# A mixture of experts that returns every expert's rows by one-hot products, with the rows for its gathers written through GpSimd's queue

## The chip, the cores and the metric

The kernel runs on one core of a Trainium2 chip. The core has a matrix engine (TensorE, PE in the rows), a vector engine (VectorE, DVE), a scalar engine (ScalarE, ACT), a general engine (GpSimd, POOL) and a sync engine (SyncE, SP) that only issues transfers. Transfers can be issued from SP's, ACT's and POOL's queues and run on 16 DMA engines. The metric is the device time of one execution in microseconds.

## The reference, cut to what matters

One layer on 512 tokens (and 16 meta tokens) of width 1,024: a mixer of two attention branches, then a mixture of 32 experts in which each token goes to two experts of one group, then a final norm. All arithmetic is float32.

```python
u = rmsnorm(h, norm_ffn_g)                  # 512 x 1024
g_sel = top_1(softmax(u @ w_group + b_group))
e_sel = top_2(softmax((u @ w_router + b_router) of that group))
gate  = p_grp * p_exp / sum(p_exp)
for each expert e, on the rows of u that chose it:
    hid = silu(x @ w1[e]) * (x @ w3[e])     # 1024 -> 512
    y   = hid @ w2[e]                       # 512 -> 1024
    out[token] += y * gate
h = h + out
return rmsnorm(h, norm_final_g)
```

## The kernel before, in words

The first half (to about 500 us) is the mixer; its instructions are placed by a scheduler that orders them by a modelled time. The rest is the expert stage, where the order of TensorE, ScalarE and VectorE is the order of the code.

Before the experts, `router_half` (L849) runs for each of the four blocks b of 128 tokens and each half nh of the width, as soon as that half of the residual stream h is done. GpSimd multiplies it by the norm's weights (L854), and ACT's queue writes the result u2 to a table `u2d` in memory (L855), eight writes of 256 KB. `choose` (L877) picks the experts, `few_rows` (L1036) makes the row indices of the first pair of experts, and `gather` (L1053) fetches those rows of `u2d` into a tile X by an indirect transfer from GpSimd's queue. Meanwhile `tables` (L945) works out, by small one-hot products, the tables for all pairs: which token sits in which slot, its gate and its norm factor. `busy` (L930) gives TensorE idle products to do in between.

Each expert has 64 slots. Two experts share one gather of 128 slots; slots that hold no token are skipped by the bounds check. The loop in `stage_moe` (L1146) runs over 32 experts, in 16 pairs, and `expert` (L1171) is one step of it: in four parts g it takes two weight pieces each and multiplies (`up_step`, L1110), and between them it does the expert before: transposes its hidden rows (L1123) and multiplies them by four w2 pieces (`down_piece`, L1131). In odd steps X is transposed for the next pair (L1095). A step reads 12 weight pieces of 512 KB, all through SP's queue, into rings of tiles: 24 tiles "R", 11 tiles "W", and 5 tiles "P" once at the start. SP issues them up to 35 pieces ahead, and each waits until the tile it goes to has been read by TensorE.

What an expert gives back goes one of two ways. `FAR = 12`: the first 12 experts (six pairs) are `far` (L1206): ScalarE and VectorE scale the two halves of the product by the gate into a tile, and for each pair `scatter` (L1066) writes its rows by an indirect transfer to a table `y2d` in memory, one row for each token and choice. The table is cleared early in the mixer by `clear_far` (L1058), four writes of 1 MB through SP's queue. `fetch_far` (L1072), at step 13, reads all of `y2d` back in eight transfers of 512 KB into eight R tiles, and step 16 adds them to h (L1196). The later 20 experts are `near` (L1232): GpSimd builds the one-hot matrix ST of tokens and slots (L1084), ScalarE and VectorE scale and split the product into a tile Y of two parts (L176, L177), and in every second step `arrived` (L1218) multiplies Y by ST for each block of 128 tokens (`to_tokens`, L1144) and adds the sums to h (L1225). ST takes a W tile, Y a P tile.

`ending` (L1240) finishes the last pair, the final norm and the output.

Of the kernel before, what the change touches and what calls it, by code (L numbers as in the profile page):

```python
# [9 lines left out]
F32 = mybir.dt.float32  # L10
# [13 lines left out]
NB = 4  # L24
# [42 lines left out]

GATES_A = [4, 4, 4, 4]
TOPK = [(3,), (2,), (1, 0), ()]
FAR = 12  # L70


class Body:
# [106 lines left out]
    def setup(self):  # L180
        nc, a = self.nc, self.a
        nc.scalar.preload_act_table_set("natural_log_exp_and_others")
        cs = self.C([128, C_ONCE], F32, "const")
        nc.scalar.dma_start(cs, a["consts"][:, 0:C_ONCE])
        self.cs = cs
        self.idt = cs[:, C_ID:C_ID + 128]
        self.idb = self.C([128, 128], BF16, "idb")
        nc.vector.tensor_copy(self.idb, self.idt)
        once = self.H([128, C_N - C_ONCE], F32, "once")
        nc.scalar.dma_start(once, a["consts"][:, C_ONCE:C_N])  # L190
        for k, (name, dt) in enumerate((("maskb", BF16), ("srope", F32R))):
            t = self.C([128, 128], dt, name)
            nc.vector.tensor_copy(t, once[:, 128 * k:128 * k + 128])
            setattr(self, name, t)
        self.tokb = self.C([128, 8], BF16, "tokb")
        nc.vector.tensor_copy(self.tokb, cs[:, C_TOKB:C_TOKB + 8])
        self.nhalf = self.C([128, 1], F32, "nhalf")
        nc.gpsimd.memset(self.nhalf, -0.5)
        self.gat = [self.dr.tile([128, 8, 512], F32, name=f"gate{i}", tag=f"gate{i}") for i in range(2)]

        self.u2d = self.dr.tile([T, D], F32, name="u2d", tag="u2d")
        self.y2d = self.dr.tile([2 * T, D], F32, name="y2d", tag="y2d")
        win = a["w_in"].rearrange("(c p) n -> p c n", p=128)

        def unit(*cols, eng=None):
            for kh in range(2):
                pc, at = [], 0
                for c0, n in cols:
                    pc.append((lambda t, at=at, n=n: t[:, :, at:at + n],
                               win[:, 4 * kh:4 * kh + 4, c0:c0 + n]))  # L210
                    at += n
                self.queue([128, 4, 256], *pc, how=dict(n=at) if at < 256 else dict(eng=eng))

        def unit128(c0):
            self.queue([128, 8, 128], (lambda t: t, win[:, :, c0:c0 + 128]), how=dict(eng=nc.gpsimd) if c0 >= O_GA else None)

        unit((O_CKV, 144), (O_KI, 72))
        unit((O_QI, 256), eng=nc.gpsimd)
        unit((O_QI + 256, 256), eng=nc.gpsimd)
        unit128(O_QA)  # L220
        unit128(O_KA)
        unit((O_VA, 256))
        unit((O_VA + 256, 256))
        self.gate_n = 0
        n = 0

        def gates(k):
            nonlocal n
            for i in range(n, n + k):
                unit128((O_GA if i < 8 else O_GB) + 128 * (i % 8))  # L230
            n += k

        def ups(w):
            v = a[w].rearrange("(c p) n -> p c n", p=128)
            for nh in range(2):
                for kp in range(2):
                    self.queue([128, 2, 512], (lambda t: t, v[:, 2 * kp:2 * kp + 2, 512 * nh:512 * nh + 512]))
                yield

        for g in range(4):  # L240
            if g < 3:
                unit128(O_QA + 128 * (g + 1))
                unit128(O_KA + 128 * (g + 1))
            else:
                unit((O_QB, 256))
                unit((O_QB + 256, 256))
            gates(GATES_A[g])
        ua = ups("w_up_a")
        for g in range(4):
            if g < 2:  # L250
                next(ua)
        ub = ups("w_up_b")
        next(ub)
        next(ub)
        v = a["w_o"].rearrange("(c p) n -> p c n", p=128)
        for nh in range(2):
            for kp in range(4):
                self.queue([128, 2, 512], (lambda t: t, v[:, 2 * kp:2 * kp + 2, 512 * nh:512 * nh + 512]))
        self.expert_at = len(self.loads)
        pcs = [self.expert_pieces(a["w1"][e], a["w3"][e], a["w2"][e]) for e in self.experts()]  # L260
        order = []
        for e in range(NE):
            last = iter(pcs[e - 1][8:] if e > 0 else [])
            for g, c in enumerate(self.spread(e)):
                order += pcs[e][2 * g:2 * g + 2]
                order += [next(last) for _ in range(c)]
        order += pcs[NE - 1][8:]
        for i, (shape, src) in enumerate(order):
            self.queue(shape, (lambda t: t, src), tile=self.home(i))
# [579 lines left out]
    def router_half(self, b, nh, h):  # L849
# [2 lines left out]
        cols = slice(512 * nh, 512 * nh + 512)  # L852
        u2 = self.H([128, 512], F32, "u2")
        nc.gpsimd.tensor_tensor(u2, h, self.g2[:, cols], ALU.mult)  # L854
        nc.scalar.dma_start(self.u2d[128 * b:128 * b + 128, cols], u2)  # L855
        junk = self.A([128, 512], F32, "junk")
        nc.scalar.activation(junk, h, AF.Square, accum_out=self.ss[:, b, nh:nh + 1])
        p = self.tr()
# [86 lines left out]
    def tables(self, d):  # L945
# [14 lines left out]
        den = self.S([128, NB], F32, "den", bufs=1)  # L960
        nc.vector.tensor_tensor(den, s[:, :, 0], s[:, :, 1], ALU.mult)
        nc.vector.reciprocal(den, den)
        self.vec = self.S([128, NB, 2, 4], F32, "vec", bufs=1)
        tok = cs[:, C_TOK:C_TOK + 8].rearrange("p (k b) -> p b k", k=2)
        nc.scalar.activation(self.vec[:, :, :, 0], tok[:, :, 0:1].to_broadcast([128, NB, 2]), AF.Copy)
        nc.scalar.activation(self.vec[:, :, :, 2], self.rs.unsqueeze(2).to_broadcast([128, NB, 2]), AF.Copy)
        nc.scalar.activation(self.vec[:, :, :, 3], tok, AF.Copy)
        nc.vector.tensor_tensor(self.vec[:, :, :, 1], d[:, :, 4:6], den.unsqueeze(2).to_broadcast([128, NB, 2]), ALU.mult)
        io = cs[:, C_I128:C_I128 + 128]
        n = [128, 8, 4, 16]  # L970
        cv = self.H(n, F32, "cv")
        nc.vector.tensor_tensor(cv, self.cb.unsqueeze(2).to_broadcast(n),
                                self.vec.rearrange("p b k n -> p (b k) n").unsqueeze(3).to_broadcast(n), ALU.mult)
        tp = self.av()[:, 0:64]
        for q in range(2):
            rh = self.H([128, 4, 128], F32, "rowoh")
            n = [128, 4, 128]
# [17 lines left out]
        nc.vector.tensor_scalar(it, self.tab[:, 0], 0.0, 4095.0, op0=ALU.is_equal, op1=ALU.mult)  # L995
        self.idx = self.C([128, 16], I32, "idx")
        nc.vector.scalar_tensor_tensor(self.idx, self.tab[:, 0], -1.0, it, op0=ALU.add, op1=ALU.add)
        self.idy = self.C([128, 16], I32, "idy")
        nc.vector.scalar_tensor_tensor(self.idy, tp[:, 48:64], -1.0, it, op0=ALU.add, op1=ALU.add)

    def overflow(self):

# [50 lines left out]
    def gather(self, x, ix, n):  # L1053
        self.nc.gpsimd.indirect_dma_start(  # L1054
            out=x[0:n], out_offset=None, in_=self.u2d[:, :],
            in_offset=bass.IndirectOffsetOnAxis(ap=ix, axis=0), bounds_check=T - 1, oob_is_err=False)

    def clear_far(self):  # L1058

        z = self.R([128, D], F32, "z")  # L1060
        self.nc.gpsimd.memset(z, 0.0)
        y = self.y2d.rearrange("(p a) d -> p a d", a=8)
        for a in range(0, 8, 2):
            self.nc.sync.dma_start(y[:, a:a + 2, :], z.unsqueeze(1).to_broadcast([128, 2, D]))

    def scatter(self, y, p):  # L1066

        self.nc.gpsimd.indirect_dma_start(
            out=self.y2d[:, :], out_offset=bass.IndirectOffsetOnAxis(ap=self.idy[:, p:p + 1], axis=0), in_=y,
            in_offset=None, bounds_check=2 * T - 1, oob_is_err=False)  # L1070

    def fetch_far(self):  # L1072

        self.back = []
        for b in range(NB):
            for k in range(2):
                t = self.R([128, D], F32, "back")
                r = T * k + 128 * b
                self.nc.gpsimd.dma_start(t, self.y2d[r:r + 128, :])
                self.back.append((self.h[b], t))  # L1080

    def tokens(self, tk, st):

# [62 lines left out]
    def stage_moe(self):  # L1146
        nc = self.nc
        self.hT = [self.H([128, 4, 64], F32, "hT") for _ in range(2)]
        with self.tc.manual_schedule(engines={nc.tensor.engine, nc.scalar.engine, nc.vector.engine}):
# [5 lines left out]
            xs = self.x_copy(self.x_turn(self.X[0]))  # L1155
            hid, self.kept = None, []
            for e in range(NE):
                if e == FAR + 1:
                    self.fetch_far()
                if e == NE - 2:  # L1160
                    self.gf = self.A([128, D], F32, "gfin")
                    nc.gpsimd.dma_start(self.gf, self.a["norm_final_g"].partition_broadcast(128))
# [8 lines left out]
    def expert(self, e, xs, hid):  # L1171
# [8 lines left out]
        for g, k in enumerate(self.spread(e)):  # L1180
# [10 lines left out]
                c += 1  # L1191
            if len(self.kept) == 2:
                self.arrived((g + 2) % 4)
            if e == FAR + 4:
                for h, back in self.back[2 * g:2 * g + 2]:
                    nc.vector.tensor_tensor(h, back, h, ALU.add)  # L1196
            if e == NE - 1 and g == 2:
                self.last = {2: (self.av(), self.mm())}
                self.stay(2)
        if len(self.kept) == 2:  # L1200
            self.kept = []
        if c == 4:
            (self.far if e - 1 < FAR else self.near)(o, e - 1)
        return nx, hid

    def far(self, o, e):  # L1206

        p, r = divmod(e, 2)
        if r == 0:
            self.y = self.P([128, D], F32, "far")  # L1210
        y = self.y[64 * r:64 * r + 64]
        gate = self.gate[:, r, p:p + 1]
        self.nc.scalar.activation(y[:, 0:512], o[0:64], AF.Copy, scale=gate[0:64])
        self.nc.vector.tensor_scalar(y[:, 512:], o[64:128], gate[64:128], None, op0=ALU.mult)
        if r:
            self.scatter(self.y, p)

    def arrived(self, b):  # L1218

# [136 lines left out]
def block_kernel(ctx: ExitStack, tc: tile.TileContext, **aps):  # L1356
# [6 lines left out]
    hp = tc.high_priority  # L1363
    aw = s.a_weights(*s.a_qk())
    s.a_values()
    s.clear_far()
    for g in range(4):
        if g < 3:
            nxt = s.a_weights(*s.a_qk())
# [59 lines left out]
```

## Time and profile before

| | us |
|---|---|
| median of 3 runs | 1030.07 (1025.9 to 1030.82) |
| the profiled execution: its time | 1029.66 |
| its span, first to last instruction | 1027.9 |
| TensorE busy | 912.8 (89% of the span) |
| VectorE busy | 514.4 (50%) |
| ScalarE busy | 340.5 (33%) |
| GpSimd busy | 203.6 (20%) |

The span is what the profile's rows are counted in; the execution's own time lies 1.8 us above it. A busy TensorE is not one at its peak, and a share over the whole span mixes stages with different limits, so the stage of the experts, from about 500 us on, is read by itself. In a row "x8" is a count, and `[3.26 <-DMA X<-u2d,ixr]` at its end says that the engine stood idle that long before it and what released it. Tile names are those of the program without buffer numbers: raw is a weight piece, X the gathered rows, mm, tr and av are tiles of the matrix engine's output memory.

### The profile page before, as it was taken

The page shows a single profiled execution, that of the slowest core. Times are in us where ns is not written, and L with a number is a line of the kernel's source. Part 1 is how long each engine was busy: PE and PEld are TensorE (multiplying, and loading weights), DVE is VectorE, ACT ScalarE, POOL GpSimd, SP SyncE. Part 2 cuts the span into 40 slices and gives each one's busy share as a digit, 9 for nine tenths or more (in the row PEclk, how much of TensorE's full clock was granted, in tenths as well). Part 3 has the DMA queues.
Part 4 walks back from the last instruction along what each step waited for, and adds up shares of the span by engine and source line. Part 5 has one row for each costly group of instructions (what it writes and reads, how often), then busy time and mean ns, then how long its engine had stood idle before and what let it go on. Part 6 is the DMA issues. An engine that isn't in the chain of part 4 may idle for free.

```text
span 1027.9 us, 13393 instructions
## 1 busy us (share of the span) xinstructions
PE 912.8 (89%) x4862; PEld 567.7 (55%) x4863; DVE 514.4 (50%) x1021; ACT 340.5 (33%) x670; POOL 203.6 (20%) x232
## 2 busy tenths in 40 slices
PE   6989999899998989889789998878749999989994
PEld 5877897778896878668543332223213433333331
DVE  7559999997827679584521141110234322223232
ACT  6156645567645576452101111111101111111113
POOL 4220042514250100252210000002212011111201
PEclk8899899899999999999889999999969999999998
DMA  9000062314433134388679999999999999999962
GB/s 318 20 21 21 22 225 62 103 42 123 131 90 103 44 110 145 81 299 311 263 285 417 416 416 416 418 417 415 414 417 417 414 415 416 416 415 417 416 281 83
DMA packets 112021, 263.57 MB, mean 256 GB/s; under 512 B 17341, under 2 KB 49349, under 8 KB 111953
## 3 DMA queue, kind: packets, MB, share of 16 engines
q1 hardware_dynamic: 95296, 237.89, 59.8%
q10 hardware_dynamic: 12192, 14.32, 4.2%
q0 software_dynamic: 4464, 10.48, 2.7%
q8 instruction: 39, 0.64, 0.2%
q14 instruction: 30, 0.24, 0.1%
HBM read 252.70 MB, written 15.73 MB: 261 GB/s over the span
## 4 chain that ended last, share of the span: by engine, by line
PE 44%; DMA 31%; DVE 15%; issue 3%; ACT 3%; POOL 3%; ACTq 0%; DVEq 0%; SPq 0%; POOLq 0%
DMA raw<-in_w 28%; PE mm L1110 11%; PE mm L1131 5%; PE mm L381 4%; PE mm L392 4%; PE mm L811 3%; PE mm L779 3%; PE mm L1144 3%; DVE E L680 2%; DVE score L548 2%; PE av L593 2%; PE mm L500 2%; DVE m L547 2%; PE mm L501 1%; DVE w L168 1%
## 5 line engine op out<-in xcount | busy, mean ns | idle before, releaser
L1110 PE MATMUL mm<-raw,xs 128*64 128x512 f32 x1024 | 249.9, 605 | 21.2 <-DMA raw<-in_w 20.9
L1110 PEld LDWEIGHTS mm<-raw,xs 128*64 128x64 f32 x1024 | 68.1, 137 | 157.5 <-issue 111.1
L1131 PE MATMUL mm<-raw,hT 128*64 128x512 f32 x512 | 130.1, 602 | 26.1 <-DMA raw<-in_w 25.6
L392 PE MATMUL mm<-uH,w 128*128 128x512 f32 (+1 forms) x448 | 129.9, 370 | 2.9 <-DVE w L168 2.7
L1116 DVE SCALAR_TENSOR_TENSOR hid<-mm,rss,g 64x512 f32<-64x512 f32 x32 | 23.8, 743 | 190.3 <-ACT g L1114 190.3
L1114 ACT ACTIVATE g<-mm,rss 64x512 f32<-64x512 f32 x32 | 21.9, 684 | 227.8 <-PE mm L1110 227.8
L1225 DVE TENSOR_TENSOR h<-mm,h 128x512 f32<-128x512 f32 x72 | 46.4, 686 | 94.0 <-PE mm L1144 94.0
L392 PEld LDWEIGHTS mm<-uH,w 128*128 128x128 f32 x448 | 81.6, 191 | 17.4 <-DVE w L168 3.1
L381 PE MATMUL mm<-w,uH 128*128 128x256 f32 (+1 forms) x448 | 86.8, 295 | 1.5 <-ACT nat L467 1.1
L1131 PEld LDWEIGHTS mm<-raw,hT 128*64 128x64 f32 x512 | 34.1, 137 | 95.0 <-issue 47.0
L392 PE MATMUL mm<-uL,w 128*128 128x512 f32 (+1 forms) x224 | 82.9, 371 | 0.0
L381 PEld LDWEIGHTS mm<-w,uH 128*128 128x128 f32 x448 | 74.2, 203 | 2.8 <-ACT nat L467 1.6
L381 PE MATMUL mm<-w,uL 128*128 128x256 f32 (+1 forms) x224 | 65.9, 294 | 2.6 <-DVE uL L174 2.6
L167 ACT ACTIVATE w<-raw 128x1024 fp32r<-128x1024 f32 (+1 forms) x54 | 55.5, 1048 | 15.0 <-DMA raw<-in_w_in 10.3
L1084 POOL TENSOR_SCALAR ST<-route,tks 128x512 fp32r<-128x512 f32 x20 | 33.1, 1662 | 131.6 <-PE mm L1110 72.7
L168 POOL TENSOR_TENSOR w<-raw,w 128x1024 fp32r<-128x1024 f32 x20 | 48.5, 2438 | 46.1 <-ACT w L167 16.2
L1054 POOL DMA_INDIRECT X<-u2d,idx x15 | 15.5, 1035 | 204.9 <-PE tr L1095 154.1
L1144 PE MATMUL mm<-Y,ST 64*128 64x512 f32 x308 | 51.6, 424 | 0.0
L168 DVE TENSOR_TENSOR w<-raw,w 128x1024 fp32r<-128x1024 f32 (+1 forms) x34 | 46.8, 1388 | 6.3 <-ACT w L167 5.5
L381 PEld LDWEIGHTS mm<-w,uL 128*128 128x128 f32 x224 | 45.3, 202 | 3.0 <-DVE uL L174 3.0
L392 PEld LDWEIGHTS mm<-uL,w 128*128 128x128 f32 x224 | 42.7, 191 | 6.8
L1144 PEld LDWEIGHTS mm<-Y,ST 64*128 64x128 f32 x308 | 30.5, 190 | 26.9 <-issue 16.2
(333 smaller groups left out, 1493.7 us busy)
## 6 DMA issues: line engine op xcount, KB each, us to landing
raw<-in_w SPq DMA_DIRECT2D x384, 512.0 KB, 10.0
raw<-in_w_in SPq DMA_DIRECT2D x36, 512.0 KB, 4.1
y2d<-z SPq DMA_DIRECT2D x4, 1024.0 KB, 9.0
gate<-gst ACTq DMA_DIRECT2D x16, 256.0 KB, 2.7
gate<-gate ACTq DMA_DIRECT2D x8, 512.0 KB, 6.4
raw<-in_w_o SPq DMA_DIRECT2D x8, 512.0 KB, 5.2
back<-y2d POOLq DMA_DIRECT2D x8, 512.0 KB, 16.6
x<-in_x SPq DMA_DIRECT2D x4, 512.0 KB, 5.8
```

Source lines behind the costliest of these rows:

```text
L167: nc.scalar.activation(h, r, AF.Copy)
L168: (eng or nc.vector).tensor_tensor(l, r, h.bitcast(F32), ALU.subtract)
L381: nc.tensor.matmul(o, s, m[:, c % 4, :n], start=(c == 0 and k == 0), stop=(c == 7 and k == 2))
L392: nc.tensor.matmul(p[:, :x1 - x0], s[:, c, :], m, start=(c == 0 and k == 0), stop=(c == 7 and k == 2))
L779: nc.tensor.matmul(p, s, y[c][:, m, :], start=(c == 0 and k == 0), stop=(c == 3 and k == 2))
L811: nc.tensor.matmul(p, s, m[:, c % 2, :], start=(c == 0 and k == 0), stop=(c == 7 and k == 2))
L1084: self.nc.gpsimd.tensor_scalar(st, self.io512, tk, None, op0=ALU.is_equal)
L1110: self.nc.tensor.matmul(p[r:r + 64], xs[:, k, par], w[:, c, :], start=(k == 0), stop=(k == 7))
L1116: self.nc.vector.scalar_tensor_tensor(hid, p[0:64], rs[0:64], g1, op0=ALU.mult, op1=ALU.mult)
L1131: self.nc.tensor.matmul(o[64 * n:64 * n + 64], ht[:, c, :], w2[:, 0, 512 * n:512 * n + 512], start=(c == 0), stop=(c == 3))
L1144: self.nc.tensor.matmul(ps[n], st[r, 128 * b:128 * b + 128], y[r, j, :], start=(first and j == 0), stop=(last and j == 1))
L1225: self.nc.vector.tensor_tensor(h, ps[n], h, ALU.add)
```

## The change

`FAR` and the three functions of the way through memory go: no clearing, no scatter, no reading back, no fourth column in the tables (the row of `y2d` that a slot goes to). All 32 experts are `near`. The eight writes of u2 move from ACT's queue to GpSimd's.

```diff
-FAR = 12
...
-        self.y2d = self.dr.tile([2 * T, D], F32, name="y2d", tag="y2d")
...
         nc.gpsimd.tensor_tensor(u2, h, self.g2[:, cols], ALU.mult)
-        nc.scalar.dma_start(self.u2d[128 * b:128 * b + 128, cols], u2)
+        nc.gpsimd.dma_start(self.u2d[128 * b:128 * b + 128, cols], u2)
...
-        self.vec = self.S([128, NB, 2, 4], F32, "vec", bufs=1)
+        self.vec = self.S([128, NB, 2, 3], F32, "vec", bufs=1)
...
-        nc.scalar.activation(self.vec[:, :, :, 3], tok, AF.Copy)
...
-        self.idy = self.C([128, 16], I32, "idy")
-        nc.vector.scalar_tensor_tensor(self.idy, tp[:, 48:64], -1.0, it, op0=ALU.add, op1=ALU.add)
...
-                if e == FAR + 1:
-                    self.fetch_far()
...
-            if e == FAR + 4:
-                for h, back in self.back[2 * g:2 * g + 2]:
-                    nc.vector.tensor_tensor(h, back, h, ALU.add)
...
         if c == 4:
-            (self.far if e - 1 < FAR else self.near)(o, e - 1)
+            self.near(o, e - 1)
...
-    s.clear_far()
```

Three places show how instructions move. The first is the last write of u2. On ScalarE before, with what each instruction waits for, the program's last two writes stand between the squares of L857 and the exponential of the gates; DMAHW2 is a count of finished transfers, and Pool and DVE count those engines' instructions.

```order
L857 ACTIVATE junk_5098,ss_4729<-h_4706 128x512 [waits DVE_49,Activation_49]
L855 DMA u2d<-u_5095 128x512 [waits DMAHW5_49,Pool_49]
L857 ACTIVATE junk_5147,ss_4729<-h_4708 128x512 [waits DVE_49,Activation_49]
L855 DMA u2d<-u_5144 128x512 [waits DMAHW2_49,Pool_49]
L942 ACTIVATE gd_5243<-gd_5243 128x24 [waits DVE_49]
```

On GpSimd in the changed kernel the same two writes stand behind the product that makes their data, and the first gather behind them.

```order
L852 TENSOR_TENSOR u_5088<-h_4699,gffn_4703 128x512 [waits DMAHW7_49,DMAHW0_49,DVE_49]
L871 TENSOR_TENSOR rs_4723<-ms_5105,nhalf_95 128x1 [waits DVE_49]
L853 DMA u2d<-u_5088 128x512 [waits Pool_49]
L852 TENSOR_TENSOR u_5137<-h_4701,gffn_4703 128x512 [waits DMASW0_49,DVE_49]
L853 DMA u2d<-u_5137 128x512 [waits Pool_49]
L871 TENSOR_TENSOR rs_4723<-ms_5154,nhalf_95 128x1 [waits DVE_49]
L1048 DMA X_4724<-u2d,ixr_5218 128x1024 [waits DMASW4_49,DMASW5_49,DMASW3_49,DMASW6_49,DMASW2_49,DMASW7_49,DMASW1_49,DVE_49]
```

The writes lost their wait for a DMAHW count. SP's weight loads of the kernel before use the same eight counts in turn; the one on DMAHW2 that is issued last ahead of that write is the first of these rows.

```order
L140 DMA raw_5376<-in_w 128x1024 [waits DMAHW2_49]
L140 DMA raw_5382<-in_w 128x1024 [waits DMAHW3_49]
L140 DMA raw_5392<-in_w 128x1024 [waits DMAHW4_49]
L140 DMA raw_5364<-in_w 128x1024 [waits DMAHW5_49,PE_49]
L140 DMA raw_5366<-in_w 128x1024 [waits DMAHW6_49,PE_49]
```

In the changed kernel the loads on SP keep these counts, without the eight writes of u2 between them.

The second place is TensorE at the start of the fourth expert's step. Before, the transposes of the expert before it are followed by the next two weight pieces.

```order
L1110 MATMUL mm_5562<-raw_5376,xs_5452 64x512
L1123 MATMUL tr_5571<-const_83,hid_5547 128x64 x4
L1110 MATMUL mm_5562<-raw_5382,xs_5452 64x512
L1110 MATMUL mm_5562<-raw_5380,xs_5452 64x512
...
L1095 MATMUL tr_5586<-const_83,X_4731 128x128 x4
```

In the changed kernel (L1080 is L1110 there, L1093 is L1123, L1114 is L1144) eight products to the tokens stand between them (four rows are shown), and so in all four parts of every second step from here on.

```order
L1080 MATMUL mm_5553<-raw_5366,xs_5442 64x512
L1093 MATMUL tr_5562<-const_83,hid_5539 128x64 x4
L1114 MATMUL mm_5569<-Y_5483,ST_5481 128x512
L1114 MATMUL mm_5570<-Y_5483,ST_5481 128x512
...
L1114 MATMUL mm_5569<-Y_5550,ST_5481 128x512
L1114 MATMUL mm_5570<-Y_5550,ST_5481 128x512
...
L1080 MATMUL mm_5553<-raw_5372,xs_5442 64x512
```

That is 32 products for each of the six pairs that were far. The third place is GpSimd's queue in the first steps: before, gathers of X and scatters to y2d.

```order
L1054 DMA X_4732<-u2d,idx_5302 128x1024 [waits DMASW1_49,PE_49]
L1068 DMA y2d<-far_5491,idy_5304 1024x1024 [waits DVE_49]
L1054 DMA X_4731<-u2d,idx_5302 128x1024 [waits DMASW2_49,PE_49]
L1068 DMA y2d<-far_5635,idy_5304 1024x1024 [waits DMASW4_49,DVE_49]
L1054 DMA X_4732<-u2d,idx_5302 128x1024 [waits DMASW3_49,PE_49]
```

In the changed kernel (L1048 is the gather, L1054 the one-hot matrix) the scatters' places hold two matrices for each pair, which wait for TensorE to leave a W tile.

```order
L1048 DMA X_4725<-u2d,idx_5294 128x1024 [waits DMASW1_49,PE_49]
L1054 TENSOR_SCALAR ST_5481<-route,tks_5279 128x512 [waits DMAHW6_49,PE_49]
L1054 TENSOR_SCALAR ST_5481<-route,tks_5279 128x512
L1048 DMA X_4724<-u2d,idx_5294 128x1024 [waits DMASW2_49,PE_49]
L1054 TENSOR_SCALAR ST_5674<-route,tks_5279 128x512 [waits DMAHW5_49,PE_49,Activation_49]
L1054 TENSOR_SCALAR ST_5674<-route,tks_5279 128x512
```

In the mixer the scheduler places a few dozen instructions of TensorE and VectorE earlier or later by some rows, and the weight splits on GpSimd by one or two; none is added there.

## Rows read from the trace of the kernel before

**Rows 1.** The page: what the DMA engines moved in 40 equal slices of the span.

```profile
GB/s 318 20 21 21 22 225 62 103 42 123 131 90 103 44 110 145 81 299 311 263 285 417 416 416 416 418 417 415 414 417 417 414 415 416 416 415 417 416 281 83
```

**Rows 2.** Busy time by stretch: length; PE, PEld, DVE, ACT, POOL; granted clock; DMA share; GB/s.

```profile
130.00:160.00 30.00, 28.64 (x208) 26.25 (x207) 29.14 (x69) 14.97 (x31) 13.67 (x10) 1.00 0.50 182
...
540.00:560.00 20.00, 20.00 (x96) 7.11 (x94) 3.00 (x4) 3.50 (x6) 1.01 (x1) 1.00 1.03 417
...
720.00:760.00 40.00, 20.04 (x96) 7.35 (x92) 6.79 (x10) 3.04 (x5) 5.41 (x9) 0.77 1.03 415
760.00:800.00 40.00, 40.00 (x199) 15.61 (x199) 20.69 (x24) 5.18 (x9) 9.33 (x5) 0.97 1.03 417
...
960.00:1000.00 40.00, 36.67 (x178) 13.00 (x174) 10.08 (x15) 4.89 (x8) 6.19 (x4) 1.00 0.86 351
```

**Rows 3.** The timeline of ACT: the gate (L1114) of experts 1, 7, 18, 24, 31.

```profile
543.85 0.68 ACT L1114 ACTIVATE g<-mm,rss 64x512 f32<-64x512 f32 x1 [5.18 <-PE mm L1110]
...
614.35 0.68 ACT L1114 ACTIVATE g<-mm,rss 64x512 f32<-64x512 f32 x1 [5.19 <-PE mm L1110]
...
800.24 0.68 ACT L1114 ACTIVATE g<-mm,rss 64x512 f32<-64x512 f32 x1 [6.33 <-PE mm L1110]
...
884.87 0.68 ACT L1114 ACTIVATE g<-mm,rss 64x512 f32<-64x512 f32 x1 [6.61 <-PE mm L1110]
...
997.30 0.69 ACT L1114 ACTIVATE g<-mm,rss 64x512 f32<-64x512 f32 x1 [12.03 <-PE mm L1110]
```

**Rows 4.** The chain that ended last: start, length, what.

```profile
739.18 19.14 DMA raw<-in_w
...
982.23 1.94 PE mm L1110 x8
```

**Rows 5.** DMA: one queue's packets, megabytes and share; issues, KB each, median us to landing.

```profile
q0 software_dynamic: 4464, 10.48, 2.7%
...
back<-y2d POOLq DMA_DIRECT2D x8, 512.0 KB, 16.6
...
u2d<-u ACTq DMA_DIRECT2D x8, 256.0 KB, 6.7
...
gfin<-in_norm_final_g POOLq DMA_DIRECT2D x1, 512.0 KB, 7.1
...
X<-u2d,idx POOLq DMA_INDIRECT x15, 7.1
```

**Rows 6.** The timeline from the last u2 to the first expert.

```profile
502.60 1.27 POOL L854 TENSOR_TENSOR u<-h,gffn 128x512 f32<-128x512 f32 x1 [4.78 <-issue]
...
509.91 0.33 ACTq L855 DMA_DIRECT2D u2d<-u  x1
...
511.75 0.16 DVE L1050 TENSOR_SCALAR ixr<-av 128x1 int32<-128x1 f32 x1 [0.47 <-PE av L1048]
...
517.67 1.29 POOL L1054 DMA_INDIRECT X<-u2d,ixr  x1 [12.26 <-DMA raw<-in_w]
...
518.36 1.89 PE L934 MATMUL mm<-route,idb 128*128 128x512 bf16 x8
...
523.51 1.97 PE L1095 MATMUL tr<-const,X 128*128 128x128 f32 x8 [3.26 <-DMA X<-u2d,ixr]
```

**Rows 7.** Busy time by stretch, as in Rows 2, around the first expert's start.

```profile
522.00:524.00 2.00, 0.49 (x3) 0.49 (x4) 0.00 (x0) 0.00 (x0) 0.00 (x0) 0.86 0.52 150
524.00:526.00 2.00, 2.00 (x9) 1.37 (x10) 0.48 (x1) 0.60 (x1) 0.25 (x1) 0.50 0.00 0
526.00:528.00 2.00, 2.00 (x10) 0.65 (x8) 0.21 (x1) 0.00 (x0) 0.75 (x1) 0.79 0.29 49
```

**Rows 8.** Groups by line: busy, mean ns of one, idle time before and its releasers.

```profile
L1225 DVE TENSOR_TENSOR h<-mm,h 128x512 f32<-128x512 f32 x72 | 46.4, 686 | 94.0 <-PE mm L1144 94.0
...
L1084 POOL TENSOR_SCALAR ST<-route,tks 128x512 fp32r<-128x512 f32 x20 | 33.1, 1662 | 131.6 <-PE mm L1110 72.7
L168 POOL TENSOR_TENSOR w<-raw,w 128x1024 fp32r<-128x1024 f32 x20 | 48.5, 2438 | 46.1 <-ACT w L167 16.2
```

More of the change, by code (lines that the diff above doesn't have):

```diff
@@ L962, in tables @@
         nc.vector.reciprocal(den, den)
-        self.vec = self.S([128, NB, 2, 4], F32, "vec", bufs=1)
-        tok = cs[:, C_TOK:C_TOK + 8].rearrange("p (k b) -> p b k", k=2)
-        nc.scalar.activation(self.vec[:, :, :, 0], tok[:, :, 0:1].to_broadcast([128, NB, 2]), AF.Copy)
+        self.vec = self.S([128, NB, 2, 3], F32, "vec", bufs=1)
+        nc.scalar.activation(self.vec[:, :, :, 0], cs[:, C_TOK:C_TOK + NB].unsqueeze(2).to_broadcast([128, NB, 2]), AF.Copy)
         nc.scalar.activation(self.vec[:, :, :, 2], self.rs.unsqueeze(2).to_broadcast([128, NB, 2]), AF.Copy)
-        nc.scalar.activation(self.vec[:, :, :, 3], tok, AF.Copy)
         nc.vector.tensor_tensor(self.vec[:, :, :, 1], d[:, :, 4:6], den.unsqueeze(2).to_broadcast([128, NB, 2]), ALU.mult)
         io = cs[:, C_I128:C_I128 + 128]
-        n = [128, 8, 4, 16]
+        n = [128, 8, 3, 16]
         cv = self.H(n, F32, "cv")
@@ L973, in tables @@
                                 self.vec.rearrange("p b k n -> p (b k) n").unsqueeze(3).to_broadcast(n), ALU.mult)
-        tp = self.av()[:, 0:64]
+        tp = self.av()[:, 0:48]
         for q in range(2):
@@ L1056, in gather @@
             in_offset=bass.IndirectOffsetOnAxis(ap=ix, axis=0), bounds_check=T - 1, oob_is_err=False)
[L1058 to L1080, printed above, removed]
     def tokens(self, tk, st):
@@ L1202, in expert @@
         if c == 4:
-            (self.far if e - 1 < FAR else self.near)(o, e - 1)
+            self.near(o, e - 1)
         return nx, hid
[L1206 to L1216, printed above, removed]
     def arrived(self, b):
```

## The prediction

> **What bounds the kernel now.** I read the bytes by slice first. Up to about 500 us they jump between 20 and 311 GB/s; from the 22nd slice to the 38th they stand at 414 to 418 [rows 1]. So the expert stage is to be looked at as a stream. The stretches say how full it is: DMA share 1.03 at 415 to 417 GB/s at 540 us, at 720 and at 760, that is, from about 540 to past 960, while TensorE is busy for 40 of 40 us in one stretch and for 20 of 40 in another [rows 2]. TensorE's load changes and the stream's doesn't: the stream sets the end. The chain agrees: it holds a wait of 19.14 us for one weight piece at 739 us, and its last wait for a weight ends at 982.23 us [rows 4]. From there on TensorE runs without one, 45.7 us to the end of the span (1027.9); I take that tail as it is.
>
> The reader should see a second thing, since it decides how safe the first is: TensorE's own pace where nothing is late. From expert 1 to 7, all far, the gates are 70.50 us apart, 23.50 a pair. From expert 18 to 24, all near, 84.63 us, 28.21 a pair [rows 3]. The stream needs more: 24 pieces of 0.524 MB and on average 64 gathered rows of 4 KB (1,024 rows in 16 gathers, two for each token) are 12.84 MB, at 416.5 GB/s 30.8 us a pair. A near pair still fits under it, by 2.6 us; a far pair by 7.3.
>
> **The way through memory: what leaves the stream.** GpSimd's queue moved 10.48 MB [rows 5]. Eight reads of y2d at 0.524 MB are 4.19, the final norm's weights 0.52, the gathers 1,024 x 4,096 bytes = 4.19. What is left, 1.57 MB, is what the six scatters wrote. The change takes 4.19 + 1.57 = 5.76 MB out of a stream that runs at 416.5 GB/s: **13.8 us**. All of it counts, because the stream is full at both places, also where the reads of y2d hold TensorE up (half busy from 720 to 760 us, clock 0.77) and where it catches up after [rows 2].
>
> **What it costs TensorE and the others.** Six pairs go from 23.50 to 28.21 us, 28 us of work in all. It lies under the stream as long as TensorE keeps ahead. Without any wait, expert 31's gate would come 15 pairs of 28.21 us after expert 1's, at 543.85 + 423.2 = 967.0 us; the stream brings it today at 997.30 [rows 3] and then at about 983. TensorE has 16 us in hand, about 1.1 us a pair. VectorE adds 48 more sums to h of 0.69 us, GpSimd 12 more one-hot halves of 1.66 us [rows 8]; in the near stretch VectorE is busy for 20.7 of 40 us and GpSimd for 9.3 [rows 2], and they do it there at the pace of 28.21, so this hides too. GpSimd's one-hot matrix can wait for a W tile, and the next gather stands behind it; near pairs have both in that order already, so I price it at nothing, and with the cover gone at what a pair then takes over 29.3 us.
>
> **The tiles.** ST now takes W tiles from the first pair on, so fewer weights can be under way. The near stretch at 760 us lives with that at 417 GB/s [rows 2]: nothing. The eight R tiles for y2d come free.
>
> **The last write of u2.** The last product of u2 ends at 502.60 + 1.27 = 503.87 us, but its write is issued at 509.91 [rows 6]. ScalarE's queue has nothing to do then; the write waits for the count of a weight load (the order of the change section shows DMAHW2). It lands at 517.67, when the gather that waited for it starts, although its indices were ready at 511.9. The gather lands 5.84 us later; TensorE, done with its idle products at 518.36 + 1.89 = 520.25, starts on X at 523.51, 3.26 us late. From GpSimd's queue the write has no such wait and goes out at about 505, counting 1.3 us for the issue like the gather's. Its landing has no row, so I bound it: 6.7 us, the median of these writes from ScalarE's queue, and 16.6, that of the eight reads of y2d, eight at once, on GpSimd's; the gathers there take 7.1 [rows 5]. One write of 256 KB is nearest to the gather: landing at 512, gather from 512 to 518, before TensorE is ready at 520.25. Landing counts only beyond 514.4. So TensorE gains 3.3 us, in the other bound (landing at 521.6) it loses 3.9.
>
> The idle gap also costs clock: after it the granted clock is 0.50 (1.2 GHz) to 526 us and 0.79 to 528 [rows 7]; over the 0.6 us that the first expert runs to 526 and the next 2 that is 0.3 + 0.4 = 0.7 us. Without the gap I count it back. These **4.0 us** reach the end only if the stream starts earlier with TensorE, and it does: the tiles are full, and DMA stands at shares of 0.52, 0.00 and 0.29 in these six us, 4.4 us of idle time, until the first expert's tiles come free [rows 7].
>
> Here a rule of the Trainium skill stands against the row. Its page "DMA: Bandwidth & Descriptors", section "Issuing engines are not separate DMA queues", says that transfers from any engine's queue run on the same 16 DMA engines, so another queue only saves the time to initiate them, usually a small thing. By that alone this term would be near 0 and the whole 13.8; by the row, the 6 us between data and issue are no matter of bandwidth and can go, so I keep the 4.0.
>
> **The rest.** The seven other writes add some 0.6 to 1.3 us each to GpSimd between products 7 us apart: hidden. One table column, one copy and one index operation leave the start, under 0.4 us: not counted. The clearing of y2d lies where VectorE is busy for 29.14 of 30 us and DMA half [rows 2]: its 4 MB hid, nothing. What the scheduler places otherwise in the mixer has no price in the trace; nearest is a weight split on GpSimd, 2.44 us [rows 8], whose place moves: 0, with two of them, 5 us, either way.
>
> **Sum.** 1029.66 - 13.8 - 4.0 = 1011.9 us, against the profiled execution's own time, which lies 0.4 us under the median of 1030.07, so the two count as one.
>
> **Rivals.**
> - *The last write lands late.* GpSimd shares the queue with nothing else then, which speaks for 7 us; the first gather's issue takes 1.29 us [rows 6], which shows that issues there can stretch. The start gives between nothing and -3.9: 1016 to 1020. The Trainium skill names a mechanism, on its page "SBUF — State Buffer", section "SBUF: two separate sides": while VectorE runs certain copies GpSimd can't write a transfer's descriptors. No run here shows it yet.
> - *The stream was not the bound.* If 13.8 us of bytes hid somewhere, only the start is left: 1025.7. A DMA share of 1.03 at every place with TensorE half idle speaks against it.
> - *TensorE becomes the bound* (the other side). Above 29.3 us a pair it sets the end; from 30.5 on the change costs time (expert 1's gate 4.0 us earlier, at 539.85, and (997.30 - 539.85) / 15); at 31.5 it is 15 us over, 1045. For it: expert stages that were far had no products to the tokens, and a late one-hot matrix would hold them up. Against it: three near pairs in a row took 28.21 each [rows 3].
> - *The mixer's other order* eats or adds more than 5 us: 1005 or 1019.
>
> **Numbers.** Forecast 0.62; late write 0.15; mixer 0.12, half each way; stream not the bound 0.06; TensorE 0.05. With the mixer's 5 us to either side the forecast holds 1006 to 1018; the late write and the late mixer reach 1020, the early mixer 1005. From 1005 to 1020.5 leaves the last two rivals and some tail out, below 2 in 10. A measurement of this kernel tells 0.5%, 5.2 us, from no change. Faster: forecast, late write, mixer, less a tenth of them, 0.84; the same: stream not the bound and that remainder, 0.11; slower: 0.05.
>
> **What would show it.** The bytes: no y2d in the list of transfers and GpSimd's queue at 4.7 MB plus the 2.1 MB of u2. The stream: 415 to 417 GB/s from about 535 to past 950, the last wait of the chain for a weight near 964. TensorE: pairs 28.2 us apart from expert 3 on, with waits for weights only from expert 20 or so. The start: last u2 issued near 505, X's transposes near 520 with no idle time before them, clock 1.00 at 522. I am wrong if DMA has holes after 540 us, if TensorE waits for ST, Y or X, if pairs take over 29.3 us, or if the start of the expert stage has moved by more than 5 us.

## The result, and the profile after

The changed kernel took 1019.25 us (median of 4 runs, 1016.69 to 1021.13), the kernel before 1030.44 us beside it (4 runs, 1025.9 to 1031.32). The ratio is 0.9899, with a 95% interval of 0.9868 to 0.993: faster by 1.0%, 10.4 us (7.2 to 13.6; the two medians alone lie 11.2 us apart). The forecast was 1011.9 us with a range of 1005 to 1020.5. So the sign and the range held, but the gain was to be 17.8 us, and 7.4 us of it are missing. The profiled execution took 1021.13 us, its span 1019.3.

First the page of the changed kernel: the bytes by slice, and the packets, megabytes and share of two DMA queues.

```profile
GB/s 302 38 22 22 22 62 42 124 32 134 92 131 73 63 124 125 63 274 371 183 359 410 408 409 408 408 408 408 409 408 409 408 407 408 409 408 410 408 269 85
...
q1 hardware_dynamic: 94208, 233.70, 60.3%
...
q0 software_dynamic: 3088, 6.82, 1.8%
```

GpSimd's queue moves 6.82 MB, the 4.7 + 2.1 that were foretold: the way through memory is gone. But the plateau from the 22nd slice on, 414 to 418 before [rows 1], now lies at 407 to 410. Even the first slice, where nothing of the experts runs, fell from 318 to 302. Busy time by stretch (the columns of rows 2) says whether the stream has holes:

```profile
522.00:524.00 2.00, 1.70 (x12) 0.89 (x12) 0.69 (x1) 0.60 (x1) 1.19 (x2) 1.00 0.96 363
524.00:526.00 2.00, 2.00 (x12) 0.62 (x10) 0.00 (x0) 0.00 (x0) 0.00 (x0) 1.00 0.63 168
526.00:528.00 2.00, 2.00 (x12) 0.67 (x10) 0.00 (x0) 0.00 (x0) 0.00 (x0) 1.00 0.88 272
540.00:560.00 20.00, 20.00 (x102) 7.88 (x100) 4.60 (x7) 4.11 (x7) 3.23 (x3) 1.00 1.03 408
720.00:760.00 40.00, 40.00 (x210) 16.23 (x208) 12.83 (x20) 6.47 (x11) 5.24 (x4) 1.00 1.03 409
760.00:800.00 40.00, 37.95 (x186) 14.22 (x182) 11.44 (x18) 5.49 (x9) 4.18 (x3) 0.96 1.03 408
```

It has none: the DMA share is 1.03 as before, and at that share fewer bytes come. The DMA engines are as busy and each transfer takes longer: in the packet records of the two traces, from 560 to 720 us, a packet of 4 KB on SP's queue took 160.0 ns on average before and 163.2 ns here. The first three stretches answer rows 7: the granted clock is 1.00 (2.4 GHz) where it was 0.86, 0.50 and 0.79, and DMA is not idle there any more.

The gates on ACT (L1084 now, L1114 before), of experts 0, 1, 17 and 31:

```profile
530.06 0.68 ACT L1084 ACTIVATE g<-mm,rss 64x512 f32<-64x512 f32 x1 [7.21 <-PE mm L1080]
540.65 0.68 ACT L1084 ACTIVATE g<-mm,rss 64x512 f32<-64x512 f32 x1 [5.19 <-PE mm L1080]
...
765.14 0.69 ACT L1084 ACTIVATE g<-mm,rss 64x512 f32<-64x512 f32 x1 [7.74 <-PE mm L1080]
...
989.30 0.69 ACT L1084 ACTIVATE g<-mm,rss 64x512 f32<-64x512 f32 x1 [12.24 <-PE mm L1080]
```

Expert 1 comes 3.2 us earlier than in rows 3; eight pairs follow in 224.5 us, 28.1 each, and the list of TensorE's waits is empty from 541 to 765 us. From then on it waits for weights, and expert 31 is only 8.0 us earlier than before. The chain that ended last (start, length, what) has its first and last waits for a weight here:

```profile
513.58 7.82 DMA X<-u2d,ixr
...
764.98 10.15 DMA raw<-in_w
...
962.50 10.18 DMA raw<-in_w
...
972.80 3.10 PE mm L1080 x8
```

The last ends at 972.68, and the product that waited starts at 972.80 (982.23 before), where the prediction had 964. Behind it lie 46.5 us to the end (45.7 before). So all but 0.8 us of the missing time is ahead of that wait.

### The profile page after: what moved, and what is told of

Its sections match the earlier page's. It is cut to its first block, busy times and chain, and to the rows that moved or that the text cites. A ratio compares the mean times of both kernels' runs of the same rounds, so it can differ in the third digit from the quotient of the medians.

```text
span 1019.3 us, 13834 instructions
## 1 busy us (share of the span) xinstructions
PE 939.9 (92%) x5054; PEld 587.0 (58%) x5055; DVE 538.1 (53%) x1060; ACT 339.4 (33%) x669; POOL 215.9 (21%) x237
## 2 busy tenths in 40 slices
DMA packets 108408, 253.66 MB, mean 249 GB/s; under 512 B 16665, under 2 KB 48673, under 8 KB 108337
## 3 DMA queue, kind: packets, MB, share of 16 engines
q1 hardware_dynamic: 94208, 233.70, 60.3%
q0 software_dynamic: 3088, 6.82, 1.8%
## 4 chain that ended last, share of the span: by engine, by line
PE 61%; DMA 17%; DVE 14%; ACT 4%; issue 2%; POOL 1%; DVEq 0%; ACTq 0%; POOLq 0%; SPq 0%
PE mm L1080 16%; DMA raw<-in_w 14%; PE mm L1101 8%; PE mm L390 7%; PE mm L1114 5%; PE mm L777 4%; PE mm L379 4%; PE mm L809 3%; DVE E L678 2%; PE av L591 2%; PE mm L498 2%; PE mm L499 1%; PE tr L1065 1%; PE tr L1093 1%; DVE score L546 1%
## 5 line engine op out<-in xcount | busy, mean ns | idle before, releaser
L1080 PE MATMUL mm<-raw,xs 128*64 128x512 f32 x1024 | 248.3, 606 | 15.4 <-DMA raw<-in_w 11.2
L1080 PEld LDWEIGHTS mm<-raw,xs 128*64 128x64 f32 x1024 | 66.9, 137 | 145.2 <-issue 109.4
L1178 DVE TENSOR_TENSOR h<-mm,h 128x512 f32<-128x512 f32 x120 | 77.3, 686 | 120.2 <-PE mm L1114 120.2
L1101 PE MATMUL mm<-raw,hT 128*64 128x512 f32 x512 | 128.0, 598 | 3.8 <-DMA raw<-in_w 3.2
L1086 DVE SCALAR_TENSOR_TENSOR hid<-mm,rss,g 64x512 f32<-64x512 f32 x32 | 23.8, 743 | 164.4 <-ACT g L1084 164.4
L1084 ACT ACTIVATE g<-mm,rss 64x512 f32<-64x512 f32 x32 | 21.9, 684 | 242.7 <-PE mm L1080 242.7
L1054 POOL TENSOR_SCALAR ST<-route,tks 128x512 fp32r<-128x512 f32 x32 | 49.9, 1565 | 184.2 <-PE mm L1080 80.8
L1114 PE MATMUL mm<-Y,ST 64*128 64x512 f32 x500 | 81.3, 418 | 0.0
L1114 PEld LDWEIGHTS mm<-Y,ST 64*128 64x128 f32 x500 | 48.5, 188 | 42.1 <-issue 24.3
L1048 POOL DMA_INDIRECT X<-u2d,idx x15 | 15.7, 1048 | 179.6 <-PE tr L1065 146.0
```

Of the source, the lines that this page charges most:

```text
L1054: self.nc.gpsimd.tensor_scalar(st, self.io512, tk, None, op0=ALU.is_equal)
L1080: self.nc.tensor.matmul(p[r:r + 64], xs[:, k, par], w[:, c, :], start=(k == 0), stop=(k == 7))
L1086: self.nc.vector.scalar_tensor_tensor(hid, p[0:64], rs[0:64], g1, op0=ALU.mult, op1=ALU.mult)
L1101: self.nc.tensor.matmul(o[64 * n:64 * n + 64], ht[:, c, :], w2[:, 0, 512 * n:512 * n + 512], start=(c == 0), stop=(c == 3))
L1114: self.nc.tensor.matmul(ps[n], st[r, 128 * b:128 * b + 128], y[r, j, :], start=(first and j == 0), stop=(last and j == 1))
L1178: self.nc.vector.tensor_tensor(h, ps[n], h, ALU.add)
```

## The experiments

**First: is the slower stream the chip's or the change's, and which part's?** Theory A was that the profiled execution met a slower chip, Theory B that the change slows the stream. Both kernels ran again unaltered, and each edit alone:

```
u2_only   (kernel before)    - nc.scalar.dma_start(self.u2d[...], u2)
                             + nc.gpsimd.dma_start(self.u2d[...], u2)
far_only  (kernel changed)   - nc.gpsimd.dma_start(self.u2d[...], u2)
                             + nc.scalar.dma_start(self.u2d[...], u2)
```

> The kernel before once more, unchanged, on the chip of the next three. Theory A (the slower stream of the changed kernel's profiled execution, 408 GB/s against 416.5, belongs to the chip or the execution, not to the change): its rate between 560 and 960 us comes out within 1 GB/s of the changed kernel's on this chip. Theory B (the change itself slows the stream): 416 GB/s here and 408 for the changed kernel. Ratio 1.000 under both.

> The changed kernel once more, on the same chip. Theory A: the same GB/s as the kernel before there, and so nearly all of the 13.8 us of bytes, plus 2 to 3 us at the start: about 14 to 17 us faster, ratio 0.984 to 0.987. Theory B: 408 GB/s against 416, about 10 us faster, ratio 0.990.

> The kernel before with the eight writes of u2 on GpSimd's queue, and nothing else changed. From the trace after, TensorE starts on the experts 2 to 3 us earlier and the stream with it. Theory A: 2 to 4 us faster, ratio 0.996 to 0.998, stream at the rate of the kernel before. Theory B, if it is GpSimd's queue that slows the stream: 408 GB/s and 5 to 7 us slower, ratio 1.005 to 1.007.

> The changed kernel with the writes of u2 back on ScalarE's queue: only the way through memory is gone. Theory A: 13 to 14 us faster than before, ratio 0.986 to 0.988, stream at the rate of the kernel before. Theory B, if it is the missing tables or tiles that slow the stream: 408 GB/s and 5 to 6 us faster, ratio 0.994 to 0.995.

Measured against the kernel before on the same chip: before_same 1029.76 us, ratio 1.0009 [0.9984, 1.0035]; after_same 1022.21, 0.9922 [0.9899, 0.9945]; u2_only 1025.7, 0.996 [0.9931, 0.9989]; far_only 1024.64, 0.9952 [0.9934, 0.9971]. The stretch from 760 to 800 us of before_same, after_same, u2_only and far_only, in that order:

```profile
760.00:800.00 40.00, 40.00 (x202) 15.24 (x200) 20.77 (x25) 5.86 (x10) 8.93 (x5) 1.00 1.03 417
```

```profile
760.00:800.00 40.00, 36.77 (x186) 14.19 (x184) 12.72 (x19) 5.47 (x9) 4.17 (x3) 1.00 1.03 408
```

```profile
760.00:800.00 40.00, 40.00 (x202) 15.17 (x200) 21.03 (x26) 5.87 (x10) 9.20 (x5) 1.00 1.03 418
```

```profile
760.00:800.00 40.00, 37.64 (x193) 14.84 (x191) 11.96 (x18) 4.70 (x8) 5.26 (x4) 1.00 1.03 408
```

On one chip the unaltered kernels ran at 417 and 408 GB/s, so A fell. The slow stream comes with the removal of the far way and not with GpSimd's queue. That was odd, since the near experts of the kernel before ran at 417 at the same place [rows 2].

The two compiled programs gave the next theories, in what they place where. The change removes `idy`, a table of 64 bytes in each partition, from the pool of constants, and every tile that is placed behind it, the weight tiles (`raw`) of the next pool among them, lies 64 bytes lower: in the compiled programs the starts of the weight tiles were multiples of 256 bytes and are now 192 over one. And with the 4 MB table `y2d` gone, the other tables in memory (`gate`, `u2d`) lie lower as well. **Theory E**: the shift of 64 bytes in SBUF slows the transfers. **Theory C**: the tables' place in memory does. A third was the mix of near instructions itself.

**Second: addresses, and nothing else.** Three kernels get a constant tile that is written once and read by nothing, ahead of `idx` in `tables`; the fourth gets `y2d` and its clearing back, never read:

```
after_pad64, before_pad64   + self.pad = self.C([128, 16], I32, "pad")
                            + nc.gpsimd.memset(self.pad, 0)
after_pad192                + self.pad = self.C([128, 48], I32, "pad")
                            + nc.gpsimd.memset(self.pad, 0)
after_table                 + self.y2d = self.dr.tile([2 * T, D], F32, name="y2d", tag="y2d")
                            + s.clear_far()
```

> The changed kernel with a 64-byte constant tile (written once by GpSimd, read by nothing) where the removed table of scatter rows stood, so that the tiles that the weights are loaded into lie at the same SBUF addresses as before (multiples of 256 bytes; in the changed kernel they lie 64 bytes lower). Theory E (the 64-byte shift slows every transfer): the stream is back at 415 to 417 GB/s instead of 408 to 409 from the first experts to the end, the first slice of the page at 314 to 318 GB/s instead of 302, and the time is 7 to 10 us below that of the changed kernel, a ratio of 0.981 to 0.985 to the kernel before. Theory C (the missing 4 MB table in memory, which moves the other tables, slows it): 408 to 409 GB/s and a ratio of 0.989 to 0.993. The same holds for a third theory, that the mix of near instructions slows it.

> The changed kernel with a constant tile of 192 bytes instead: the weight tiles then lie at multiples of 128 bytes that are no multiples of 256. If, by theory E, multiples of 128 are enough, 415 to 417 GB/s and a ratio of 0.981 to 0.985; if only multiples of 256 do, 408 to 412 GB/s and a ratio of 0.986 to 0.993. By theory C 408 to 409 GB/s and 0.989 to 0.993.

> The kernel before with one more 64-byte constant tile (written once, read by nothing), which moves its weight tiles 64 bytes up, off the multiples of 256 and of 128 bytes; nothing else is changed. Theory E: its stream falls from 415 to 417 to 408 to 409 GB/s and it is slower by 8 to 11 us, a ratio of 1.007 to 1.011. Theory C and the theory of the instruction mix: no change, 415 to 417 GB/s and a ratio within 0.3% of 1.

> The changed kernel with the 4 MB table in memory declared and cleared at the start as before, but never read, so that the tables in memory lie at the addresses of the kernel before while the SBUF tiles stay 64 bytes lower. Theory C: 415 to 417 GB/s and a ratio of 0.981 to 0.988 (the 4.2 MB of clearing may cost some of it). Theory E: 408 to 409 GB/s and a ratio of 0.989 to 0.996.

Measured: after_pad64 1011.09 us, ratio 0.9808 [0.9783, 0.9833]; after_pad192 1010.53, 0.9804 [0.9783, 0.9826]; before_pad64 1040.05, 1.0099 [1.008, 1.0119]; after_table 1021.6, 0.9906 [0.9879, 0.9933]. The bytes by slice of each, in that order:

```profile
GB/s 317 26 22 22 22 64 43 125 32 136 61 164 51 86 125 126 64 218 391 156 360 416 415 417 414 415 417 414 415 415 414 414 414 415 416 416 416 415 297 85
```

```profile
GB/s 322 21 22 22 22 64 43 125 32 136 62 163 53 84 125 126 64 174 396 161 375 399 418 419 419 419 419 418 419 419 418 417 419 418 418 419 420 417 286 85
```

```profile
GB/s 302 32 21 21 41 203 81 81 81 87 166 49 102 70 86 141 134 297 264 319 290 409 409 409 410 410 410 408 408 408 407 407 407 408 408 407 409 409 262 82
```

```profile
GB/s 298 41 21 21 22 227 49 117 42 124 109 113 34 101 124 124 63 225 389 166 361 410 408 409 408 409 408 408 408 409 409 407 408 408 407 409 409 407 297 84
```

Theory E holds in both directions: 64 bytes of padding give the changed kernel its 415 GB/s back, and 64 bytes in the kernel before, where nothing else is altered, take them away and cost it 10.2 us (0.0099 x 1029.54; 8.2 to 12.3). With the table back in memory and the tiles low the stream stays at 408: Theory C fell, and the mix of instructions with it, as the padded kernel runs the same mix. That 128 over a multiple of 256 is as good as a multiple was open; it is, with 417 to 420 GB/s, even a little above the 415 to 417 that were expected, and in time the two can't be told apart.

With the stream as the prediction assumed it, its other steps can be read. Waits of the chain of after_pad64:

```profile
512.67 7.62 DMA X<-u2d,ixr
...
954.04 9.99 DMA raw<-in_w
```

The last wait for a weight ends at 964.03. Its gates of experts 1, 17, 20 and 31 (L1086 here):

```profile
539.56 0.68 ACT L1086 ACTIVATE g<-mm,rss 64x512 f32<-64x512 f32 x1 [5.18 <-PE mm L1082]
...
764.13 0.68 ACT L1086 ACTIVATE g<-mm,rss 64x512 f32<-64x512 f32 x1 [7.73 <-PE mm L1082]
...
805.61 0.68 ACT L1086 ACTIVATE g<-mm,rss 64x512 f32<-64x512 f32 x1 [7.52 <-PE mm L1082]
...
979.23 0.68 ACT L1086 ACTIVATE g<-mm,rss 64x512 f32<-64x512 f32 x1 [12.03 <-PE mm L1082]
```

Eight unhindered pairs take 224.57 us, 28.07 each, and the first gate held up by a weight is expert 20's: the idle time before it is 7.52 us, where those of the even experts from 4 to 18 have 6.61.

**Third: the bytes alone, and a finer start.** far_only_pad64 is far_only with the tile of 64 bytes, so that only the removal of the far way remains; after_pad32 is the changed kernel with a tile of 32 bytes (`[128, 8]`), its weight tiles 224 over a multiple of 256.

> The changed kernel with the u2 writes back on ScalarE's queue, as before, and with the 64-byte constant tile that puts the weight tiles back on multiples of 256 bytes: the far way's removal alone, with its 5.76 MB and without the shift. If the prediction's term of 13.8 us for these bytes is right, the stream runs at 414 to 417 GB/s, the last wait for a weight ends about 14 us earlier than before, near 965, and the ratio is 0.985 to 0.988; the other change (GpSimd's queue) is then worth what lies between this run and the changed kernel with the same tile (0.9808), some 4 to 5 us. Rival: part of the bytes' gain hangs on the earlier start, or the bytes were partly hidden, and the ratio is 0.989 to 0.993.

> The changed kernel with a constant tile of 32 bytes: its weight tiles then start at multiples of 32 bytes that are no multiples of 64 (160 over a multiple of 256? no: 224 over one). If every start off the multiples of 128 costs alike, 407 to 410 GB/s and a ratio of 0.989 to 0.993; if finer starts cost more, below 406 GB/s and a ratio above 0.993; if the loss at 64 bytes was peculiar to that offset, 414 GB/s or more and a ratio of 0.981 to 0.985.

Measured: far_only_pad64 1016.95 us, ratio 0.9858 [0.9833, 0.9883]; after_pad32 1018.98, 0.989 [0.9864, 0.9916]. Stretches from 760 to 800 us of the first and of the second:

```profile
760.00:800.00 40.00, 40.00 (x208) 15.63 (x204) 13.52 (x21) 5.38 (x9) 5.26 (x4) 1.00 1.03 415
```

```profile
760.00:800.00 40.00, 37.34 (x190) 14.37 (x188) 12.72 (x19) 5.83 (x10) 4.18 (x3) 1.00 1.03 408
```

The removal alone gives 14.7 us (0.0142 x 1031.77; 12.1 to 17.2), which agrees with all 13.8 us of the bytes counting, and the rival that much of them was hidden fell. One sign was missed: its last wait for a weight was expected to end near 965.

```profile
961.18 9.99 DMA raw<-in_w
```

It ends at 971.17, 10.9 us earlier than before (982.10, with the product behind it at 982.23 [rows 4]); the last u2 product came 1.45 us later there (504.05 against 502.60), which leaves 12.4 us. A start at a multiple of 32 costs what one at a multiple of 64 does, no more.

## Why the prediction was right, and where it was off

**The bytes** (5.76 MB, 13.8 us). Right in mechanism and, within the noise, in size: 14.7 us with the tiles where they were. What failed is an assumption under this step, that the stream goes on "at 416.5 GB/s"; the 415 to 417 GB/s that the prediction named as its sign did not come. The change moved the tiles by 64 bytes and the whole stream, not only the part taken out, ran at 408 to 409. From about 535 to 973 us, 438 us, a rate 1.9% lower (8 of 416.5) is 8.4 us; the last weight wait is 8.65 us later than in after_pad64 (972.68 against 964.03). On one chip the padded kernel and the one with low tiles and the table differ by 10.1 us (0.9906 - 0.9808, of 1029.54), and before_pad64, where nothing else changes, loses 10.2. That covers the 7.4 us that were missing; it is more than them, as the two terms of the sum came out, within their noise, somewhat larger than forecast. No term of the sum and no rival had it; the diff shows it only to a reader who asks which allocation stands behind a removed one.

**The last write of u2** (4.0 us). Right in mechanism, near in size. u2_only alone gives 4.1 us (0.004 x 1031; 1.1 to 7.1), far_only_pad64 and after_pad64, from two chips, differ by 0.0050, 5.2 us. The traces tell it with less scatter when the time is counted from the start of the last u2 product to expert 1's gate, which leaves out when the mixer ends: 41.25 us before (502.60 to 543.85), 37.19 in the changed kernel (503.46 to 540.65), 4.06 less. Over all twelve traces it is 41.2 to 41.9 us in the five with the write on ScalarE's queue and 36.4 to 37.2 in the seven with it on GpSimd's, on average 4.7 less. The changed kernel's timeline answers rows 6:

```profile
503.46 1.26 POOL L852 TENSOR_TENSOR u<-h,gffn 128x512 f32<-128x512 f32 x1 [4.20 <-DVE h L811]
...
505.02 0.58 POOL L853 DMA_DIRECT2D u2d<-u  x1 [0.30 <-POOL u L852]
...
513.13 0.16 DVE L1044 TENSOR_SCALAR ixr<-av 128x1 int32<-128x1 f32 x1 [0.47 <-PE av L1042]
...
513.58 1.20 POOL L1048 DMA_INDIRECT X<-u2d,ixr  x1 [7.29 <-DVE gd L939]
518.77 1.89 PE L932 MATMUL mm<-route,idb 128*128 128x512 bf16 x8
...
521.44 1.16 PE L1065 MATMUL tr<-const,X 128*128 128x128 f32 x8 [0.78 <-DMA X<-u2d,ixr]
```

The write goes out 0.30 us after its data instead of 6 us, and the gather follows the indices by 0.29 us (so in all seven traces; in the other five it is 6.0 to 6.5 and 5.7 to 6.2 us): the write is no longer what it waits for, and the rival of the late write fell. Some sizes were off. The indices came at 513.29 instead of about 511.9; 0.86 us of that is the mixer's later end, the rest lies between the last product and the indices. The gather took 7.82 us, not 5.84; the stream was full during all of it (DMA share 1.02 to 1.03 in every 2 us from 514 to 522), while in the kernel before the stream had run out by the gather's end [rows 7]; but that this is the reason is argued, not shown. So TensorE still stood idle for 0.78 us, not 0, which gives 2.5 us and not 3.3. The clock gave back more than the 0.7 us foretold: from X's transposes to expert 1's gate 20.34 us became 19.21. The prediction counted the slow clock from the first expert's products on and left out the transposes, 1.97 us before [rows 6] and 1.16 here. The remaining 0.4 us of the 4.06 is that the idle products end sooner after the last u2 product. That expert 1's gate came only 3.2 us earlier is the mixer's end, 0.86 us later. In far_only_pad64, with the write on ScalarE's queue, the old wait is there again:

```profile
504.05 1.27 POOL L852 TENSOR_TENSOR u<-h,gffn 128x512 f32<-128x512 f32 x1 [4.82 <-issue]
...
511.63 0.33 ACTq L853 DMA_DIRECT2D u2d<-u  x1
513.20 0.16 DVE L1046 TENSOR_SCALAR ixr<-av 128x1 int32<-128x1 f32 x1 [0.47 <-PE av L1044]
...
519.08 1.30 POOL L1050 DMA_INDIRECT X<-u2d,ixr  x1 [12.22 <-DMA raw<-in_w]
```

Data at 505.32, issue at 511.63, and the gather 5.7 us after its indices. The rule that was weighed against this term, that all queues share the same DMA engines and another queue saves little ("DMA: Bandwidth & Descriptors" of the Trainium skill, section "Issuing engines are not separate DMA queues"), holds for the bandwidth: u2_only streams at 418 GB/s. It doesn't price a wait ahead of the issue, which was the gain here.

**TensorE and the others** (nothing). Right: near pairs of 28.1 us from the start, no wait for ST or, after expert 0's 0.78 us, for X, and the rival in which TensorE becomes the bound is out. Of TensorE's waits in the changed kernel from 520 us on, weights end 14.4 us; 3.1 us in two waits are put down to Y, which the prediction had named as a sign against it:

```profile
PE mm L1080 <- DMA raw<-in_w: 11.2, 11, 2.1
PE mm L1101 <- DMA raw<-in_w: 3.2, 6, 0.6
PE mm L1080 <- DVE Y L176: 3.1, 2, 1.6
```

The columns are us in total, times and the longest; the list's four other waits, for h, X, hT and xs, are 0.3 to 0.8 us each. Both waits for Y stand at the products of a new weight (L1080), at 814 and 877 us, where the stream already sets the pace, so a weight wait behind them may take up what they cost, which is argued; whether Y or a weight really ended them no run tells apart. VectorE's sums, 48 more of them, have still a mean of 686 ns:

```profile
L1178 DVE TENSOR_TENSOR h<-mm,h 128x512 f32<-128x512 f32 x120 | 77.3, 686 | 120.2 <-PE mm L1114 120.2
```

**The mixer's other order** (nothing, two-sided 5 us). The last u2 product starts at 503.46 in the changed kernel and at 502.60 before [rows 6]; run again, the same two have it at 502.28 and 499.62. In the four traces of kernels built on the one before it lies at 499.62 to 504.50, in the eight built on the changed one at 500.97 to 507.56, the latest in after_table. One kernel alone moves by 3 us from one execution to the next, so no run separates the new order from that scatter: this stays open. The clearing of y2d, which the prediction also priced at nothing, is back in after_table: its ratio of 0.9906 can't be told from the changed kernel's 0.9899 and 0.9922.

**The sum.** With the weight tiles on multiples of 256 bytes the last wait for a weight ends at 964.03 (the prediction: near 964) and the time is 1011.09 us (1011.9). Against the kernel before on that chip this is a gain of 19.8 us (0.0192 x 1029.54; 17.2 to 22.3) where 17.8 were forecast. As the change stands, some 10 us of it are lost again to the term that was missing. That the range still held the time is luck: its bounds were set for other causes, and a slower stream had no chance of its own. Two slips lie beside the sum. The 0.84 for faster is 0.05 below the 0.89 of its three cases, about a twentieth and not "a tenth of them"; and the slices that "jump between 20 and 311 GB/s" leave out the first, 318, the one that told later that the slower stream isn't the experts' alone. after_pad64 and after_pad192 beat both kernels, by 1.9 to 2.0% against the kernel before; which of them is better isn't settled.

## What to carry to other kernels

Where a stream of transfers sets the time, price a change also by what it does to the addresses of the tiles that the stream fills: a small constant added or removed in a pool ahead of them moves all of them. Compare the plateau of GB/s before and after at an equal DMA share; a share at its top doesn't say that the stream runs at its best rate, and a first slice that falls too (318 to 302) says that the cause isn't in the stage that was changed. One dummy tile restores the old addresses and separates this effect from the change itself.

## What the runs showed of the hardware

The rate of the full stream went by where the weight tiles start in SBUF (bytes over a multiple of 256, from the compiled programs; pieces of 4 KB in each partition; DMA share 1.02 to 1.03 in all of them; GB/s of the page's slices 23 to 37):

```
start  kernels                                                  GB/s
   0   before, before_same, u2_only, after_pad64,
       far_only_pad64                                           413 to 419
 128   after_pad192                                             417 to 420
  64   before_pad64                                             407 to 410
 192   the changed kernel, after_same, far_only, after_table    407 to 410
 224   after_pad32                                              407 to 410
```

Starts at multiples of 128 bytes run some 2% faster than starts off them, and how far off made no difference that these runs show. The packet records of the same traces say how the loss is spread. A packet of 4 KB on SP's queue took 160.0 to 160.4 ns on average at starts of 0 (560 to 720 us), 159.3 at 128, and 162.9 to 163.3 at 64, 192 and 224. A packet of 512 bytes on the same queue, in the first 25 us, took 29.4 to 29.9 ns, 27.1, and 32.8 to 32.9. So, against a start of 0, one off the multiples of 128 cost some 3 ns a packet at either size, 2% of a packet of 4 KB and some 10% of one of 512 bytes. The Trainium skill, on "DMA: Bandwidth & Descriptors", section "How a descriptor splits into AXI transactions", gives the vendor's account of how a transfer is split: a read starts at a multiple of 256 bytes, so one off it fetches the bytes below its start as well and pays for them. Here the starts that moved are those written to, of which it says nothing. A loss off the multiples of 256 agrees in sign with these runs, but by that rule a start at 128 would pay as well, and it ran at 417 to 420 GB/s: the measurement decides. Why a start costs what it does no run shows. Nor is it separated which tiles count: the padding moves the weight tiles and all others behind it together. SP's queue, nearly all of it weight pieces, moved 233.70 of the 253.66 MB, and its own packets took longer.
